# Products of a zero tile ahead of the first row tile, and another landing time for the first transfers in the planner

## The chip, the cores and the metric

One NeuronCore of a Trainium2 chip runs the kernel; one launch computes one decoder layer for 1024 tokens. The metric is the device time of an execution in microseconds (us), the median of several. A profile of one execution shows what each engine did: TensorE (PE, with its weight loads as PEld), VectorE (DVE), ScalarE (ACT), GpSimd (POOL), and SyncE (SP), which issues the transfers.

## The reference

The layer has 1024 rows (tokens) of 1024 columns. What matters here is its beginning: a row-wise normalisation of `x` and the product with `w_in`.

```
def rmsnorm(x, g):
    y = x * lax.rsqrt(jnp.mean(x * x, axis=-1, keepdims=True) + EPS)
    return y * g

a = rmsnorm(h, ln_pre_mix)               # h = x, (1024, 1024)
q, k, v, u, z = jnp.split(a @ w_in, splits, axis=-1)
attn = dilated_attention(q, k, v)
sgu = spatial_gating(u, z, sgu_ln_g, sgu_ln_b, w_spatial, b_spatial)
groups = jnp.concatenate([rmsnorm(attn, attn_out_norm), rmsnorm(sgu, sgu_out_norm)], axis=-1)
h = h + rmsnorm(groups @ w_out, ln_post_mix)
g, up = jnp.split(rmsnorm(h, ln_pre_ffn) @ w_gate_up, 2, axis=-1)
h = h + rmsnorm((silu(g) * up) @ w_down, ln_post_ffn)
h = h + sigmoid(h @ w_pe_gate + b_pe_gate) * (p @ w_pe_proj)
```

## The kernel before, in words

**How it is written and ordered.** `hybrid_block` does not issue instructions. It records every operation in a `Graph` (`G.call`, with `pe` and `load` as short forms for TensorE and for a transfer), with the buffers that the operation reads and writes. When all is recorded, `Graph.order` simulates the five engines with a price for each operation (`price`) and picks, for each engine whenever it is free, the first recorded operation that is ready and whose buffers fit; `Graph.issue` then writes the instructions in the picked order, all from line 383, which is why every row of the profile names L383. What an engine gets is therefore a fixed list, which it works off in order. A transfer is planned to land at `dma + 3.0` us (line 328), where `dma` is the time at which the planned transfers before it and its own bytes are through. Buffers come from pools that are named in the profile: `m` (4 KB per partition), `s` (2 KB), `t` (a few columns), `p` (a bank of PSUM), `c` (constants).

**The beginning of the program.** The gain row `ln_pre_mix` is loaded into one partition (`g_raw`, an `m`), and a row of ones (`ones`, an `s` of one partition, set by a memset on DVE) spreads it over 128 partitions: two f32 products `ones` x `g_raw` of 512 columns each (line 622), which DVE copies from PSUM into `g_pre` (line 623). The profile shows each f32 product of this kind as two records of 512 columns. After the gain row, SP issues row tile 0 of `x` (128 rows, 512 KB), the identity `ident`, row tile 1, the four blocks of `w_in` for the values (512 KB each) and further row tiles between them.

`x_chain(t)` (line 627) treats a row tile: ACT squares it and sums the squares, ACT and POOL make the reciprocal root from the sum (`rstd_from`, the POOL row `t<-t,c`), DVE scales the two halves of the tile by it and by `g_pre` (the `SCALAR_TENSOR_TENSOR` rows), and `Feat.first` turns each half with four transposes on PE against `ident` (rows `p<-c,s`, 128x128; "turns" below). ACT copies the two turned halves from PSUM for later use (`COPY m<-p`), then casts them to the rounded type in which PE multiplies (four `CAST m<-p`), and DVE subtracts to keep the remainder (four `TENSOR_TENSOR m<-p,m`). `split_raw` does the same for a block of `w_in`: a cast on ACT (`CAST m<-m`) and a subtraction on DVE or POOL (`TENSOR_TENSOR m<-m,m`). `v_out` then multiplies: three products for each pair of such parts, 512 columns wide (rows `MATMUL p<-m,m`).

On ACT's list the first cast of `w_in` stands ahead of the two copies of row tile 0, the four casts of the turned tile stand behind the copies, and behind these the cast of the second half of the same block, which POOL's first subtraction reads.

Of the kernel before, what the change touches and what calls it, by code (L numbers as in the profile page):

```python
# [17 lines left out]
P = 128  # L18
# [95 lines left out]
class Graph:  # L114
# [109 lines left out]
    def order(self):  # L224
        ops = self.ops
        n = len(ops)
# [17 lines left out]
        port, dma, table, lanes = 0.0, 1.5, 0, [0.0] * 8  # L244
# [4 lines left out]
        def release(o):  # L249
            ready = {}  # L250
            for e in o.engines:
                ready[e] = max([d.end + (LATENCY[e] if d.engine != e else 0.0) for d in o.deps], default=0.0)
                if e in ("tensor", "vector") and o.deps:
                    own = [d for d in o.deps if d.engine == e]
                    other = [d.end + LATENCY[e] for d in o.deps if d.engine != e]
                    ready[e] = max(other + [d.start + d.cost[e][0] for d in own], default=0.0)
                    o.sure = max(other, default=-1.0) + self.MARGIN
                heapq.heappush(coming, (ready[e], o.rank, o.i, e))
                heapq.heappush(events, ready[e])
                if e == "tensor":  # L260
                    heapq.heappush(events, ready[e] + self.MARGIN)
            o.ready = ready
# [19 lines left out]
        def pick(e, now):  # L282
            best = None
            front = ops[first]
            for rank, i in waiting[e][: self.LOOK[e]] + [(front.rank, first)] * ((front.rank, first) in waiting[e]):
                o = ops[i]
                if o.port[e] and port > now + 1e-9:
                    continue
                if best is not None and o.sure > now:
                    continue  # L290
                if not fits(o, now):
                    continue
                if e != "tensor" or o.sure <= now:
                    return o
                best = o
            return best
# [6 lines left out]
        while left:  # L303
            if not events:
                raise ValueError(f"stuck at {ops[first].what} {first}")
            now = heapq.heappop(events)
            while events and events[0] <= now + 1e-9:
                heapq.heappop(events)
            while coming and coming[0][0] <= now + 1e-9:
                _, rank, i, e = heapq.heappop(coming)  # L310
                if ops[i].start is not None:
                    continue
                bisect.insort(waiting[e], (rank, i))
            for e in engines:
                if at[e] > now + 1e-9 or not waiting[e]:
                    continue
                o = pick(e, now)
                if o is None:
                    continue
                busy, took = o.cost[e]  # L320
                o.start, o.engine = now, e
                picked.append(o)
                if o.table and o.table != table:
                    busy, took, table = busy + 1.4, took + 1.4, o.table
                at[e] = now + busy
                if e == "sync":
                    dma = max(dma, now + 0.4) + o.bytes / 330e3
                    o.end = dma + 3.0
                    lanes = lanes[1:] + [o.end]
                    at[e] = max(at[e], lanes[0])  # L330
                else:
                    o.end = now + took
                if o.port[e]:
                    port = o.end
                    heapq.heappush(events, port)
                for x in o.engines:
                    if (o.rank, o.i) in waiting[x]:
                        waiting[x].remove((o.rank, o.i))
                o.new = [b for b in o.bufs if b.slot is None]
                for b in o.new:  # L340
                    b.slot = heapq.heappop(free[b.kind])[1]
                    group[b.group] = group.get(b.group, 0) + 1
                    b.ahead = first
                    early[b.kind][first : b.born] += 1
                for b in o.bufs:
                    b.left -= 1
                    b.until = max(b.until, o.end)
                    if not b.left:
                        heapq.heappush(free[b.kind], (b.until, b.slot))
                        group[b.group] -= 1  # L350
                        live[b.kind][b.born : b.last + 1] -= 1
                        early[b.kind][b.ahead : b.born] -= 1
                        heapq.heappush(events, b.until)
                done[o.i] = True
                left -= 1
                while first < n and done[first]:
                    first += 1
                for u in o.users:
                    u.waits -= 1
                    if not u.waits:  # L360
                        release(u)
                heapq.heappush(events, at[e])
                heapq.heappush(events, now + 0.02)
# [25 lines left out]
def hybrid_block(ctx: ExitStack, tc, a, out):  # L389
    G = Graph()  # L390

    def M(dt=F32, shape=(P, 1024), group=None):
        return G.buf("M", shape, dt, group)

    def SM(dt=F32, shape=(P, 512), group=None):
        return G.buf("S", shape, dt, group)

    def PB(shape=(P, 512), group=None):
        return G.buf("P", shape, F32, group)
# [10 lines left out]
    def pe(what, *args, **kw):  # L410
        return G.call("tensor", what, *args, **kw)
# [4 lines left out]
    def load(dst, src, rate=1.0):  # L416
        o = G.call("sync", "dma_start", dst, src)
        o.bytes /= rate
        return o
# [179 lines left out]

    x = a["x"][0]  # L600
    g_raw, g_pre = M()[:1, :], M()
    ones = SM()[:1, :P]
    G.call("vector", "memset", ones, 1.0)
    load(g_raw, a["ln_pre_mix"])
    xts = {}

    def x_load(t):
        xts[t] = M()
        load(xts[t], x[t * P : (t + 1) * P, :])
# [7 lines left out]
    wv_raw.append(load_raw(piece_a(w_in, 1024, 1), None))  # L617
    for t in range(4, 6):
        x_load(t)
    for cs in (LO, HI):  # L620
        ps = PB()
        pe("matmul", ps, ones, g_raw[:, cs], start=True, stop=True)
        G.call("vector", "tensor_copy", g_pre[:, cs], ps)

    A = Feat()

# [218 lines left out]
    def unit(pr, hh, Pq, vs, bias):  # L845
# [21 lines left out]
        for b in range(0, len(order), 3 if Pq == 2 else 2):  # L867
            ps = PB((P, 4, P), "turn")
            places, n = [], 0
            for j in order[b : b + (3 if Pq == 2 else 2)]:  # L870
                for ii in sorted(blocks[j]):
                    pe("transpose", ps[:, n + ii - min(blocks[j]), :], blocks[j][ii], ident)
                places.append((j, min(blocks[j]), n, len(blocks[j])))
                n += len(blocks[j])
            eh, el = SM(F32R, (P, 4, P)), SM(F32R, (P, 4, P))
            split(*(v.flat()[:, : n * P] for v in (eh, el, ps)))
            for j, i0, at, w in places:
                for s, ee in ((0, eh), (1, el)):
                    pe("matmul", po[:, i0 * P : (i0 + w) * P], vs[j], ee.flat()[:, at * P : (at + w) * P],
                       start=j == order[0] and s == 0, stop=j == order[-1] and s == 1)  # L880
# [343 lines left out]
    for q in ORDER:  # L1224
# [3 lines left out]
        for g in range(NG):  # L1228
            for j, c in USED.get(q, ()):
                cs = slice(c * 512, (c + 1) * 512)  # L1230
# [5 lines left out]
            if g % 2 == 0:  # L1236
                n = min(2, NG - g)
# [102 lines left out]
```

## Time and profile before

| | |
|---|---|
| median of 3 runs | 1178.31 us (1178.01 to 1178.48) |
| the profiled execution | 1178.0 us |
| its span, first to last instruction | 1176.2 us |
| PE busy | 1163.5 us, 99% of the span |
| DVE, ACT, POOL busy | 869.0, 576.3, 57.0 us |
| PE's share of the chain that ended last | 95% |

The span is the time in the trace; the execution's own time is 1.8 us longer. The busy time of an engine says how full it is, not what it holds up. For a change at the start of the program the views to read are the chain that ended last in its first part, which tells what released what, and the timeline of each engine over the first 15 us, where every row has its start, its length, the engine, the operation with its tiles, a count, and in brackets the idle time ahead of it with what ended it. Rows with the same operation that follow each other are merged, and the count says how many there are.

### The profile page before, as it was taken

How to read it: one execution, taken by the hardware profiler on the slowest of the kernel's cores; microseconds unless marked ns; L12 is line 12 of the kernel's file. 1: busy time of each engine (PE TensorE's matmuls, PEld its weight loads, DVE VectorE, ACT ScalarE, POOL GpSimd, SP SyncE). 2: the span in 40 equal slices, each digit the busy share in tenths (PEclk: the TensorE clock that was granted, in tenths of full speed). 3: DMA queues.
4: the chain of work that ended last, by engine and by line, in shares of the span. 5: the costliest groups of instructions: out<-in, count | busy, mean ns of one | idle time of the engine just before them, and what ended most of it. 6: DMA issues, size and time to landing. Idle time of an engine off the chain costs nothing.

```text
span 1176.2 us, 16341 instructions
## 1 busy us (share of the span) xinstructions
PE 1163.5 (99%) x5633; PEld 972.4 (83%) x5633; DVE 869.0 (74%) x1703; ACT 576.3 (49%) x1300; POOL 57.0 (5%) x68
## 2 busy tenths in 40 slices
PE   8999999999999999999999999999999999999998
PEld 6887888788878888888888888888888888888887
DVE  7888796566666676799888888887668965479653
ACT  8663436578768666566223222222344445357121
POOL 2101000000121000310000000000000000002000
PEclk9999999999999999999999999999999999999999
DMA  8224136999763996388455656544397223643111
GB/s 295 81 72 122 58 134 192 323 296 310 250 215 88 286 264 179 109 267 256 146 194 186 196 189 186 171 133 162 112 382 254 95 92 113 240 162 143 47 43 54
DMA packets 161244, 208.77 MB, mean 177 GB/s; under 512 B 12477, under 2 KB 89609, under 8 KB 161162
## 3 DMA queue, kind: packets, MB, share of 16 engines
q1 hardware_dynamic: 161162, 207.74, 55.4%
q8 instruction: 44, 0.72, 0.3%
q14 instruction: 38, 0.31, 0.1%
HBM read 147.63 MB, written 60.06 MB: 177 GB/s over the span
## 4 chain that ended last, share of the span: by engine, by line
PE 95%; DVE 2%; ACT 1%; DMA 1%; issue 0%; SPq 0%; POOL 0%; DVEq 0%; ACTq 0%
PE p L383 95%; DVE s L383 1%; ACT m L383 1%; DMA m<-in_w_in 1%; DVE t L383 1%; DMA d<-m 0%; DVE m L383 0%; SPq L383 0%; POOL m L383 0%; ACT s L383 0%; ACT t L383 0%; DVEq L383 0%; ACTq L383 0%
## 5 line engine op out<-in xcount | busy, mean ns | idle before, releaser
L383 PE MATMUL p<-m,m 128*128 128x512 f32 (+2 forms) x4620 | 1065.6, 388 | 1.9 <-DVE m L383 1.3
L383 PEld LDWEIGHTS p<-m,m 128*128 128x128 f32 x4620 | 848.0, 188 | 169.8 <-ACT m L383 2.0
L383 DVE TENSOR_TENSOR m<-m,m 128x512 fp32r<-128x512 f32 (+2 forms) x465 | 313.2, 707 | 70.5 <-ACT m L383 65.0
L383 ACT CAST m<-m 128x512 fp32r<-128x512 f32 x363 | 212.7, 622 | 192.8 <-PE p L383 148.1
L383 DVE TENSOR_TENSOR s<-p,s 128x512 f32<-128x512 f32 (+4 forms) x222 | 143.0, 655 | 85.9 <-PE p L383 58.4
L383 ACT ACTIVATE s<-s 128x512 f32<-128x512 f32 (+1 forms) x71 | 44.3, 626 | 218.0 <-DVE s L383 162.3
L383 DVE TENSOR_TENSOR m<-p,m 128x256 fp32r<-128x256 f32 (+3 forms) x132 | 61.5, 493 | 41.2 <-PE p L383 21.5
L383 POOL TENSOR_TENSOR t<-t,c 128x1 f32<-128x1 f32 (+1 forms) x56 | 42.0, 755 | 1012.4 <-ACT t L383 1002.9
L383 ACT COPY s<-p 128x512 f32<-128x512 f32 (+1 forms) x122 | 62.2, 517 | 44.0 <-PE p L383 43.0
L383 ACT CAST m<-s 128x256 fp32r<-128x256 f32 (+1 forms) x121 | 53.6, 480 | 29.3 <-PE p L383 15.6
L383 DVE TENSOR_TENSOR s<-s,s 128x512 f32<-128x512 f32 x88 | 60.7, 692 | 4.6 <-ACT s L383 0.7
L383 DVE TENSOR_TENSOR m<-s,m 128x256 fp32r<-128x256 f32 (+1 forms) x121 | 58.4, 511 | 6.9 <-ACT m L383 6.5
L383 PE MATMUL p<-c,m 128*128 128x128 f32 x328 | 49.7, 273 | 0.0
L383 ACT COPY m<-p 128x512 f32<-128x512 f32 (+1 forms) x72 | 31.5, 452 | 32.1 <-PE p L383 30.9
L383 PE MATMUL p<-c,s 128*128 128x128 f32 (+2 forms) x249 | 42.6, 282 | 2.4 <-DVE s L383 2.0
L383 PEld LDWEIGHTS p<-c,m 128*128 128x128 f32 x328 | 39.5, 140 | 5.9
L383 PE MATMUL p<-s,m 128*128 128x128 f32 (+1 forms) x256 | 43.8, 276 | 0.0
L383 ACT ACTIVATE m<-m 128x1024 f32<-128x1024 f32 x32 | 34.1, 1068 | 19.5 <-DVE m L383 15.0
L383 PEld LDWEIGHTS p<-c,s 128*128 128x128 f32 (+2 forms) x249 | 32.0, 145 | 11.4 <-DVE s L383 4.0
L383 PEld LDWEIGHTS p<-s,m 128*128 128x128 f32 x256 | 38.1, 190 | 3.2
L383 ACT ACTIVATE m<-m,t 128x384 f32<-128x384 f32 (+2 forms) x64 | 36.7, 578 | 4.9 <-DVE t L383 4.3
L383 ACT CAST m<-p 128x256 fp32r<-128x256 f32 (+1 forms) x80 | 34.4, 498 | 6.7 <-PE p L383 5.7
(58 smaller groups left out, 513.9 us busy)
## 6 DMA issues: line engine op xcount, KB each, us to landing
d<-s SPq DMA_DIRECT2D x149, 256.0 KB, 2.8
m<-d SPq DMA_DIRECT2D x51, 512.0 KB, 4.2
m<-in_w_gate_up SPq DMA_DIRECT2D x88, 256.0 KB, 3.9
m<-d SPq DMA_DIRECT2D x87, 256.0 KB, 7.2
s<-d SPq DMA_DIRECT2D x56, 256.0 KB, 4.2
d<-m SPq DMA_DIRECT2D x28, 512.0 KB, 5.4
m<-in_w_down SPq DMA_DIRECT2D x44, 256.0 KB, 6.1
m<-in_w_in SPq DMA_DIRECT2D x20, 512.0 KB, 3.9
```

The costliest lines, as they stand in the source:

```text
L383: getattr(getattr(nc, o.engine), o.what)(*[real(v) for v in o.args], **{k: real(v) for k, v in o.kw.items()})
```

## The change

A tile `unused` of 128x512 zeros is set by a memset on DVE. A new helper, `keep_busy(n)`, multiplies the tile by itself `n` times (f32, 512 columns) into a bank of PSUM that nobody reads. It is called once ahead of the two products with `ones`, and twice behind them; the latter are recorded to come after the second product with `ones`. In the planner, a transfer that is issued in the first 12 us of the plan lands 1.7 us after its bytes in place of 3.0.

```
@@ Graph.order @@
                     dma = max(dma, now + 0.4) + o.bytes / 330e3
-                    o.end = dma + 3.0
+                    o.end = dma + (3.0 if now > 12 else 1.7)
                     lanes = lanes[1:] + [o.end]
...
@@ hybrid_block @@
     g_raw, g_pre = M()[:1, :], M()
-    ones = SM()[:1, :P]
+    ones, unused = SM()[:1, :P], SM()
+    G.call("vector", "memset", unused, 0.0)
     G.call("vector", "memset", ones, 1.0)
     load(g_raw, a["ln_pre_mix"])
     xts = {}
+
+    def keep_busy(n, after=()):
+
+        ps = PB()
+        for _ in range(n):
+            pe("matmul", ps, unused[:, :P], unused, start=True, stop=True, after=after)
...
     for t in range(4, 6):
         x_load(t)
+    keep_busy(1)
     for cs in (LO, HI):
         ps = PB()
-        pe("matmul", ps, ones, g_raw[:, cs], start=True, stop=True)
+        o = pe("matmul", ps, ones, g_raw[:, cs], start=True, stop=True)
         G.call("vector", "tensor_copy", g_pre[:, cs], ps)
+    keep_busy(2, [o])
```

TensorE at the start of the program, before. In the names, `s_144` is `ones`, `m_142` is `g_raw`, `c_73` is `ident`; the first two groups of four are the turns of row tile 0.

```order
L383 MATMUL p_161<-m_142,s_144 128x512
L383 MATMUL p_163<-m_142,s_144 128x512
L383 MATMUL p_188<-c_73,s_184 128x128 x4
L383 MATMUL p_201<-c_73,s_186 128x128 x4
L383 MATMUL p_214<-c_73,s_205 128x128 x4
L383 MATMUL p_227<-m_199,m_220 128x512
```

TensorE at the same place, now. `s_144` is here `unused`, and `s_148` is `ones`.

```order
L383 MATMUL p_150<-s_144 128x512
L383 MATMUL p_163<-m_142,s_148 128x512
L383 MATMUL p_167<-m_142,s_148 128x512
L383 MATMUL p_176<-s_144 128x512 x2
L383 MATMUL p_195<-c_73,s_191 128x128 x4
L383 MATMUL p_208<-c_73,s_193 128x128 x4
L383 MATMUL p_221<-c_73,s_212 128x128 x4
L383 MATMUL p_234<-m_206,m_227 128x512
```

One product of zeros stands ahead of the products with `ones`, two stand between these and the turns of row tile 0; the rest of the list is that of before.

VectorE at the start of the program, before: the memset of a constant, that of `ones`, the two copies of the gain row, the scaling of row tile 0.

```order
L383 MEMSET c_72 128x8
L383 MEMSET s_144 1x128
L383 COPY m_165<-p_161 128x512
L383 COPY m_165<-p_163 128x512
L383 SCALAR_TENSOR_TENSOR s_184<-m_146,t_177,m_165 128x512
```

VectorE at the same place, now.

```order
L383 MEMSET c_72 128x8
L383 MEMSET s_144 128x512
L383 MEMSET s_148 1x128
L383 COPY m_169<-p_163 128x512
L383 COPY m_169<-p_167 128x512
L383 SCALAR_TENSOR_TENSOR s_191<-m_146,t_184,m_169 128x512
```

The memset of `unused` stands ahead of that of `ones`; nothing else on VectorE moves. The lists of ScalarE, GpSimd and SyncE are row for row those of before, with other buffer numbers, and they are so too with the landing of 3.0 left as it was.

## Rows read from the trace of the kernel before

**Rows 1.** The page, busy time of each engine, share of the span and number of instructions.
```profile
PE 1163.5 (99%) x5633; PEld 972.4 (83%) x5633; DVE 869.0 (74%) x1703; ACT 576.3 (49%) x1300; POOL 57.0 (5%) x68
```

**Rows 2.** The chain that ended last, in order of time, its first 60 us: start, length, what.
```profile
2.49 7.05 DMA m<-in_w_in
9.54 0.02 issue
9.56 3.21 ACT m L383 x8
12.78 0.07 issue
12.85 1.29 POOL m L383
14.14 0.04 issue
14.18 45.85 PE p L383 x224
```

**Rows 3.** The timeline of the first 22 us, rows of ACT from the first cast of weights on, and POOL's first subtraction: start, length, engine, line, operation, count, idle time before it and its releaser.
```profile
9.56 0.62 ACT L383 CAST m<-m 128x512 fp32r<-128x512 f32 x1 [0.92 <-DMA m<-in_w_in]
10.09 1.07 ACT L383 COPY m<-p 128x512 f32<-128x512 f32 x2
...
11.04 1.21 ACT L383 CAST m<-p 128x256 fp32r<-128x256 f32 x4
...
12.10 1.71 ACT L383 CAST m<-m 128x512 fp32r<-128x512 f32 x3
...
12.85 1.28 POOL L383 TENSOR_TENSOR m<-m,m 128x512 fp32r<-128x512 f32 x1 [3.56 <-ACT m L383]
...
13.65 1.12 ACT L383 COPY m<-p 128x512 f32<-128x512 f32 x2
```

**Rows 4.** The same timeline, rows of PE and, where they show single records, of its weight loads.
```profile
2.43 3.75 PE L383 MATMUL p<-m,s 1*128 1x512 f32 x4 [2.43 <-DMA m<-in_ln_pre_mix]
...
3.42 0.33 PEld L383 LDWEIGHTS p<-m,s 1*128 1x128 f32 x1 [0.52 <-issue]
...
4.27 0.33 PEld L383 LDWEIGHTS p<-m,s 1*128 1x128 f32 x1 [0.52 <-issue]
...
7.62 1.97 PE L383 MATMUL p<-c,s 128*128 128x128 f32 x8 [1.44 <-DVE s L383]
...
10.12 1.11 PE L383 MATMUL p<-c,s 128*128 128x128 f32 x4 [0.53 <-DVE s L383]
...
11.48 1.22 PE L383 MATMUL p<-m,m 128*128 128x512 f32 x2 [0.24 <-ACT m L383]
...
12.50 1.05 PE L383 MATMUL p<-c,s 128*128 128x128 f32 x4
...
13.21 8.98 PE L383 MATMUL p<-m,m 128*128 128x512 f32 x36
```

**Rows 5.** Windows of 2 us: length, busy time and instructions of PE, PEld, DVE, ACT, POOL, the granted clock of TensorE as a share of full speed, the share of the DMA engines, GB/s.
```profile
2.00:4.00 2.00, 1.57 (x2) 0.83 (x3) 0.00 (x0) 0.01 (x1) 0.00 (x0) 1.00 0.82 259
...
8.00:10.00 2.00, 1.59 (x8) 1.19 (x6) 0.91 (x2) 1.05 (x4) 0.56 (x1) 1.00 1.05 411
10.00:12.00 2.00, 1.63 (x5) 1.22 (x6) 1.43 (x3) 2.00 (x7) 0.00 (x0) 1.00 1.02 415
```

**Rows 6.** The timeline of PE from 14.6 to 40 us.
```profile
14.18 8.00 PE L383 MATMUL p<-m,m 128*128 128x512 f32 x34
22.02 0.60 PE L383 MATMUL p<-c,s 128*128 128x128 f32 x4
...
25.22 1.03 PE L383 MATMUL p<-c,s 128*128 128x128 f32 x8
```

**Rows 7.** The timeline of the first 22 us, rows of DVE up to the scaling of row tile 1, and POOL's first row of the reciprocal root.
```profile
0.81 0.07 DVE L383 MEMSET c<- 128x8 f32 x1 [0.81 <-PEq L1328]
0.85 0.17 DVE L383 MEMSET s<- 1x128 f32 x1
...
4.51 0.69 DVE L383 COPY m<-p 128x512 f32<-128x512 f32 x1 [3.50 <-PE p L383]
...
6.22 0.69 DVE L383 COPY m<-p 128x512 f32<-128x512 f32 x1 [1.01 <-PE p L383]
6.22 0.55 POOL L383 TENSOR_TENSOR t<-t,c 128x1 f32<-128x1 f32 x1 [5.78 <-ACT t L383]
...
6.83 1.41 DVE L383 SCALAR_TENSOR_TENSOR s<-m,t,m 128x512 f32<-128x512 f32 x2
...
9.32 0.75 DVE L383 SCALAR_TENSOR_TENSOR s<-m,t,m 128x512 f32<-128x512 f32 x1 [1.09 <-POOL t L383]
```

## The prediction

> **What bounds the kernel now.** I read the page's busy line first. TensorE (PE) is busy for 1163.5 of 1176.2 us [rows 1], so a change at the start can gain only what PE loses there, and it can cost whatever delays the point from which PE never waits again. The second view is the chain that ended last, over its first 60 us [rows 2]. The reader should see what stands ahead of PE's first long stretch: the transfer of a block of `w_in` (2.49 to 9.54), eight ScalarE (ACT) instructions from 9.56, one GpSimd (POOL) subtraction from 12.85 to 14.13, and then PE from 14.18. No PE instruction stands in that chain before 14.18.
>
> The third view is the timeline, taken engine by engine. ACT waits 0.92 us for the block of `w_in`, starts at 9.56, and from there on its rows touch or overlap: a cast of weights, two copies of the turned row tile out of PSUM (10.09), four casts of it (11.04), and three casts of weights (12.10) [rows 3]. The first of those three makes the weights' second half, and POOL's 1.28 us subtraction waits for it. PE's rows before 14.18 [rows 4] are short bursts: the four records of the two products with `ones` (2.43 to 6.18), the eight turns of row tile 0 (7.62 to 9.59), the four turns of 10.12, two products, four turns, three products.
>
> The clock of these bursts has to be read from their pace. The column of the granted clock says 1.00 for these stretches [rows 5], but eight turns take 1.97 us at 7.62 [rows 4] and the same eight-turn row takes 1.03 us at 25.22; four take 1.11 or 1.05 early and 0.60 at 22.02 [rows 6]. That is a factor of nearly two between equal rows, so I read the early stretch as the lower level, 1.2 GHz, up to the turns of 12.50 at least, and 2.4 GHz in the 34 products from 14.18, which follow each other every 0.235 us (8.00 us over 34) [rows 6].
>
> **The change part by part.** *The landing in the planner.* The 1.7 in place of 3.0 moves a due time in the planner and no instruction: the order on all five engines is that of before, except for the memset on VectorE (DVE) and the three products on PE. It costs and gains nothing.
>
> *The memset of the zero tile.* It stands on DVE ahead of the memset of `ones`. 8 columns took 0.07 us and 128 took 0.17 [rows 7]: 0.10 us for 120 columns, so 512 columns come to 0.49 us by the slope and to 0.68 by four times the larger row. I take 0.5, because the slope leaves the fixed part in once. The memset of `ones` then ends near 1.5 (at most 1.7), and what hides it is the landing of `ln_pre_mix`, for which PE waits until 2.43 [rows 4]. Cost: nothing.
>
> *The first zero product.* It waits for that memset, so it starts at 0.85 + 0.5 + 0.05 = 1.4 (at most 1.55). Behind it in PE's queue stand the two products with `ones`. One f32 product is two records here (four for two [rows 4]). From PE's start at 2.43 to the weight load of 3.42 are 0.99 us and to the next 0.85, so one product takes 1.84 at the lower clock and ends at 3.25 to 3.4. The `ones` products therefore start 0.8 to 0.95 late; I take 0.85. The last result comes at 7.03 in place of 6.18, the second copy of `g_pre` on DVE [rows 7] starts at 7.07 in place of 6.22, and the two scalings of row tile 0 start at 7.67 in place of 6.83, since DVE takes its instructions in order. Turns could then begin at 8.47 in place of 7.62. If the clock rises while the `ones` products run, this shrinks, but it can gain nothing: the scaling also needs POOL's power, which runs from 6.22 to 6.77 [rows 7].
>
> *The two later zero products.* They are four records: 4 x 0.85 = 3.4 us at 1.2 GHz, half of it, 1.7, at 2.4. They start where the last `ones` record lets PE go: 4.27 + 0.85 + 0.85 = 5.97 before, 6.82 with the delay. PE is free for the turns at 10.2 if nothing has risen, and at w + (10.2 - w)/2 if the clock rises at time w.
>
> *Who waits for the turns.* ACT's copies at 10.09 and, half of 1.07 later, at 10.6 [rows 3] read the eight turns. Before, the turns ended at 9.59, behind which the first copy could have run; it did not, because the weights' cast in front of it waited for its transfer. So faster or earlier turns do not start the copies earlier. With the turns at the higher clock (four in 0.60, eight in 1.03) they are in time if PE is free by 9.5. That is w + (10.2 - w)/2 = 9.5, so w = 8.8: **if the clock has risen by 8.8, the edit costs nothing.** What of PE's later rows before 14.18 becomes faster ends earlier and waits for POOL's 14.13 as before. The gain there is nothing too: PE's start at 14.18 has POOL, ACT and the transfer behind it, none of which PE feeds late.
>
> *Sum.* 0 + 0 + 0 - 0 against the profiled execution's 1178.0 us (span 1176.2 and 1.8 around it), so 1178.0 by its own account. The three runs shown have a median of 1178.31, that is 0.3 above it, and reach from 1178.01 to 1178.48. I forecast **1178.2**: no change, between the two.
>
> **The rivals.** *The clock stays low, and the zero products are late (slower).* The `ones` records kept PE without a gap for 3.75 us, and the turns after them still ran at 1.2 GHz [rows 4]; so that the f32 products of zeros raise it is not shown by any row. Then PE is free at 10.2, the first four turns end 1.11 later at 11.3, the eight 1.97 later at 12.2, and the second copy starts at 12.2 in place of 10.6. ACT, POOL and PE's 14.18 move by 1.6: **1179.6** from the profiled execution, 1179.9 from the median. It decides from w = 8.8 upwards. It passes 0.2% (2.36 us) only if the clock also stays low after PE's new start at 15.8: products at half pace until 17.3 would add the missing 0.76. Against this rival: PE would now work without a gap from 1.4 on, 7.4 us by the point that decides, and in the trace the clock rose between the turns of 12.50 and the products of 14.18, after a stretch from 10.12 on with one gap of 0.24 [rows 4, 6].
>
> *The rise is late in other executions of before (faster).* In the profiled one the clock was up by the products of 14.18, just in time. Where it rises d later, PE does half the work in d and loses d/2, and an engine kept busy from 1.4 would not. The runs shown bound it: the slowest is 0.47 above the fastest, so d is at most about 0.9, and against the median the gain is 0.3: **1178.0**; a median one microsecond lower would need d near 2, which no run shown has. The Trainium skill ("TensorE: Matmul & The Clock Gate", Part 1: The HAM clock gate) has a rule for this: the throttled clock is the default, activity releases it, and the same kernel is seen with different numbers of slow matmuls from run to run. By that rule this rival holds for some executions and the spread of before would narrow; the trace has one execution and cannot show it.
>
> *The turns are on the path after all (faster).* Then PE's rows between 10.12 and 14.18, 1.11 + 1.22 + 1.05 + 0.97 (13.21 to 14.18) = 4.35 us at the lower clock, would halve: 2.2 us, **1175.8** by the profiled execution. Against it speak ACT's rows without a gap from 9.56 and the chain, which names no PE before 14.18 [rows 2, 3].
>
> *The change does not do what it says.* As to the order this is so for the landing, as told above: it changes no row. That is in the forecast already and makes no time of its own.
>
> **How the numbers follow.** Forecast (no change, 1178.0 to 1178.6): 0.55. Zero products late (1178.7 to 1180.7, with the middle at 1179.6 to 1179.9): 0.26, of which 0.05 go beyond 0.2%. Late rise in before (1177.0 to 1178.0): 0.13. Turns on the path: 0.03. Left over: 0.03, other waits of the start that I have not seen, of either sign. A measurement of this kernel can tell about 0.2%, 2.36 us, from no change. So faster by over 0.2%: 0.03; slower by over 0.2%: 0.05; within: 0.92. The range takes in the late rise down to 1177.3 and the late zero products up to 1180.0 (1.6 above the median, and 0.1 for the dearer memset), and leaves some 0.2 outside.
>
> **What would show it.** Right: in the profile after, PE works from about 1.4; the eight turns take near 1.03 us and end by 10.6; ACT's first weight cast still starts at about 9.56 and its copies follow without a gap; POOL's subtraction and PE's long stretch still start near 12.85 and 14.18. The clock rising by 8.8 shows as weight loads or turns at half the spacing. Wrong: an idle gap on ACT between its weight cast and its copies, ended by PE (the late zero products), with PE's long stretch starting after 15; or the long stretch starting well before 14.18, which would mean that the chain named the wrong engine; or ACT's first cast starting at another time, since no term of mine moves the transfer.

## The result, and the profile after

| | before | changed |
|---|---|---|
| median | 1178.25 us (17 runs, 1177.18 to 1180.51) | 1181.22 us (17 runs, 1179.92 to 1184.48) |
| ratio to before | | 1.0024, 95% interval 1.0016 to 1.0031 |
| the profiled execution | 1178.0 | 1180.71 |
| its span | 1176.2 | 1178.9 |

The change costs 2.8 us by the ratio (1.9 to 3.7 by its interval), 3.0 by the medians. The forecast was no change, 1178.2, and its range ended at 1180.0. The ratios here and below leave out one run of e7_front that took 3833 us.

The timeline of the changed kernel's first 22 us, rows of PE and of those who wait for it, answers to [rows 3, 4, 7]; the columns are the same.

```profile
0.94 0.61 DVE L383 MEMSET s<- 128x512 f32 x2
...
1.49 2.08 PE L383 MATMUL p<-s 128*128 128x512 f32 x2 [1.49 <-DVE s L383]
...
3.49 3.78 PE L383 MATMUL p<-m,s 1*128 1x512 f32 x4
...
7.20 3.78 PE L383 MATMUL p<-s 128*128 128x512 f32 x4
7.30 0.69 DVE L383 COPY m<-p 128x512 f32<-128x512 f32 x1 [1.02 <-PE p L383]
...
8.53 0.62 ACT L383 CAST m<-m 128x512 fp32r<-128x512 f32 x1 [0.74 <-DMA m<-in_w_in]
...
10.77 2.75 PE L383 MATMUL p<-c,s 128*128 128x128 f32 x12
...
11.87 0.59 ACT L383 COPY m<-p 128x512 f32<-128x512 f32 x1 [2.72 <-PE p L383]
...
12.72 0.59 ACT L383 COPY m<-p 128x512 f32<-128x512 f32 x1 [0.27 <-PE p L383]
...
14.20 0.60 PE L383 MATMUL p<-c,s 128*128 128x128 f32 x4
...
15.00 1.27 POOL L383 TENSOR_TENSOR m<-m,m 128x512 fp32r<-128x512 f32 x1 [6.58 <-ACT m L383]
...
16.33 5.97 PE L383 MATMUL p<-m,m 128*128 128x512 f32 x25 [0.85 <-POOL m L383]
```

PE has no idle time from 1.49 to 13.5, and its records go at the pace of the lower level: the four records of the later zero products take the same 3.78 us as the four of the products with `ones`, and twelve turns take 2.75 us (0.21 each), until four turns at 14.20 take 0.60. The turns start at 10.77 in place of 7.62. ACT, which before had no gap behind its first cast of weights, now idles 2.72 and 0.27 us ahead of its two copies, both times until PE. From there everything is shifted by the same amount: the second copy from near 10.6 (the second half of the row at 10.09) to 12.72, POOL's subtraction from 12.85 to 15.00, PE's long stretch from 14.18 to 16.33, the last two by 2.15 us. PE looks fuller, and that says nothing: the page has it busy 1168.2 us against 1163.5 [rows 1].

```profile
PE 1168.2 (99%) x5639; PEld 973.6 (83%) x5639; DVE 868.9 (74%) x1704; ACT 576.7 (49%) x1300; POOL 56.7 (5%) x68
```

The chain that ended last in the first 60 us of the changed kernel answers to [rows 2].

```profile
2.49 6.02 DMA m<-in_w_in
...
8.55 6.42 issue
...
15.00 1.28 POOL m L383
16.29 0.04 issue
16.33 43.84 PE p L383 x215
```

Here the chain misleads: it follows POOL's wait on ACT to an "issue" of 6.42 us. The timeline shows what fills it: ACT waiting for the turns, that is for PE's zero products. The span grew by 2.7, and 2.15 of it lie ahead of the long stretch.

The transfer of the first block of `w_in` landed at 8.5 here and at 9.54 in the trace of before, though nothing ahead of it on SP's list changed. This turns out to matter below.

### The profile page after: what moved, and what is told of

Its sections match the earlier page's. It is cut to its first block, busy times and chain, and to the rows that moved or that the text cites. A ratio compares the mean times of both kernels' runs of the same rounds, so it can differ in the third digit from the quotient of the medians.

```text
span 1178.9 us, 16356 instructions
## 1 busy us (share of the span) xinstructions
PE 1168.2 (99%) x5639; PEld 973.6 (83%) x5639; DVE 868.9 (74%) x1704; ACT 576.7 (49%) x1300; POOL 56.7 (5%) x68
## 4 chain that ended last, share of the span: by engine, by line
PE 94%; DVE 2%; DMA 1%; ACT 1%; issue 1%; SPq 0%; POOL 0%; ACTq 0%; POOLq 0%; DVEq 0%
PE p L383 94%; DVE s L383 1%; ACT m L383 1%; DMA m<-in_w_gate_up 1%; DMA m<-in_w_in 1%; DVE t L383 1%; DMA d<-m 0%; DVE m L383 0%; SPq L383 0%; POOL m L383 0%; ACT s L383 0%; ACT t L383 0%; ACTq L383 0%; POOLq L383 0%; DVEq L383 0%
```

## The experiments

For each: the median, the ratio to before with its 95% interval, and from the profile of one of its runs the start of ACT's first cast of weights (right behind the landing of the first block of `w_in`), of the turns of row tile 0, and of PE's long stretch. Each ratio is to runs of before taken in the same series, whose medians were 1178.07 to 1178.25 (1178.52 for e9_casts_first).

| run | median us | ratio (interval) | ACT's cast | turns | long stretch |
|---|---|---|---|---|---|
| before, first trace | | | 9.56 | 7.62 | 14.18 |
| b_again | one run | | 8.68 | 7.64 | 13.29 |
| changed, first trace | 1181.22 | 1.0024 (1.0016 to 1.0031) | 8.53 | 10.77 | 16.33 |
| a_again | one run | | 8.90 | 10.42 | 15.16 |
| e0_landing | 1178.06 | 1.0003 (0.9994 to 1.0012) | 8.42 | 7.52 | 13.14 |
| e1_first | 1178.82 | 1.0007 (0.9998 to 1.0015) | 8.55 | 8.71 | 14.33 |
| e2_later | 1179.61 | 1.0018 (1.0009 to 1.0027) | 8.96 | 9.60 | 14.89 |
| e3_four | 1181.67 | 1.0036 (1.0024 to 1.0049) | 9.16 | 12.26 | 16.99 |
| e4_data | 1181.20 | 1.0027 (1.0017 to 1.0036) | 8.97 | 10.77 | 16.04 |
| e5_rounded | 1180.99 | 1.0021 (1.0012 to 1.0030) | 8.57 | 10.78 | 16.33 |
| e7_front | 1180.30 | 1.0016 (1.0006 to 1.0025) | 8.47 | 10.52 | (14.51) |
| e8_one_later | 1178.83 | 1.0005 (0.9996 to 1.0014) | 8.92 | 7.91 | 13.53 |

(e6_turns, whose zero turns share a row with the real ones, and e9_casts_first are told in their places. In e7_front PE does not wait for POOL, and its last burst starts at 14.51.)

**e0_landing: the planner's half alone.**

```
-                    o.end = dma + 3.0
+                    o.end = dma + (3.0 if now > 12 else 1.7)
```

> Only the planner's landing time is changed (1.7 in place of 3.0 for the first 12 us), no product of zeros. Theory (the loss is the zero products on PE's list, ahead of the turns): the lists of all engines are those of before, so the time is that of before, 1178.3, ratio 1.000 within 0.001, and PE's long stretch starts near 14.2. Rival (the other landing itself costs): 1179.5 or more.

1178.06 against 1178.07 of before: the landing time in the planner costs nothing that can be told (the interval ends at 1.4 us). The rows of every engine in its trace stand in the order of before, so it is also a further trace of the lists of before.

**e1_first and e2_later: one call of `keep_busy` each.**

e1_first:

```
-    keep_busy(2, [o])
```

> The change with the first zero product alone; the two later ones are left out. Theory: the products with ones come 1.06 us late, the turns begin near 8.7 in place of 7.6, their eighth ends near 10.4, and ACT's second copy, at 10.6 before, hardly waits; PE's long stretch starts at 14.0 to 14.4, time 1178.3 (at most 1178.7). Rival (the late gain row is part of the loss): a third to a half of the loss stays, 1179.3 or more, with DVE's scaling as the releaser.

e2_later:

```
-    keep_busy(1)
```

> The change with the two later zero products alone; the first is left out. Theory: all at 1.2 GHz, the zero products start at 6.14 and free PE at 9.7, 1.06 before the changed kernel; the second copy starts at 11.7, PE's long stretch at 15.3; 1.1 us above before, 1179.4. Rival (the loss is not PE's queue but the products as such): as the changed kernel, 1181. A rise of the clock before 9 would give 1178.3.

The run e2_later is near its theory: turns at 9.60, 1179.61, and by the ratio 2.1 us above before, where the theory had 1.1, the lower end of the interval. The run e1_first is between theory and rival: 1178.82, with 1.0 within the interval. ACT's copies waited 0.69 and 0.27 us for the turns, since the block landed at 8.5 in that execution; the long stretch at 14.33 is about a microsecond later than the 13.14 and 13.29 of the traces of before with a landing near it. With a landing at 9.54 ACT's copies could not run before 10.09, so the same late turns would cost next to nothing; that is worked out, and no trace of e1_first has it. By the ratios the two halves cost 0.8 and 2.1 us, which add up to the 2.8 of the whole as well as the intervals can tell.

ACT in the first 17.5 us of e1_first:

```profile
9.86 0.59 ACT L383 COPY m<-p 128x512 f32<-128x512 f32 x1 [0.69 <-PE p L383]
10.71 0.59 ACT L383 COPY m<-p 128x512 f32<-128x512 f32 x1 [0.27 <-PE p L383]
```

**e3_four: four later zero products.**

```
-    keep_busy(2, [o])
+    for i in range(4):
+        z = pe("matmul", ps, unused[:, :P], unused, start=True, stop=True, after=[o])
+        z.cost = z.cost if i < 2 else {"tensor": (0.001, 0.001)}
```

> The change with four later zero products in place of two (the two more are priced at next to nothing in the planner, so that the lists stay as they are otherwise). Theory with the clock held low by them until the end: turns 3.4 us later than in the changed kernel, PE's long stretch at 19.7, 5.6 us above before, 1183.8. With the clock rising near 13.4 as in both traces: long stretch at 18.4, 1182.5. Rival (PE's queue does not decide): as the changed kernel, 1181.

1181.67, below both numbers: the clock rose during the zero products, sooner than in the first trace of the changed kernel. The eight records took 5.23 us (below), where four take 3.78 at the lower level and eight would take 7.2, so the last 2 us of them ran at double pace and the rise is near 10.3. By the time alone the rival is not out, since the interval (1.0024 to 1.0049) overlaps that of the changed kernel (1.0016 to 1.0031). The trace decides: the turns start at 12.26, 1.5 to 1.8 later than in the two traces of the changed kernel, ACT's first copy waits 3.12 us for them, and the long stretch starts at 16.99 in place of 16.33 and 15.16. PE's queue decides.

PE and ACT in the first 17.5 us of e3_four:

```profile
7.20 5.23 PE L383 MATMUL p<-s 128*128 128x512 f32 x8
...
12.26 1.47 PE L383 MATMUL p<-c,s 128*128 128x128 f32 x12
...
12.90 1.07 ACT L383 COPY m<-p 128x512 f32<-128x512 f32 x2 [3.12 <-PE p L383]
```

**e4_data, e5_rounded, e6_turns: other work in the zero products' place.** None of the results is read by anybody.

e4_data:

```
-    keep_busy(2, [o])
+    for _ in range(2):
+        pe("matmul", ps, xts[0][:, :P], xts[0][:, LO], start=True, stop=True, after=[o])
```

> The two later products multiply row tile 0 of x by itself in place of zeros, still f32; nobody reads the result. Theory Z (the zeros are why the clock stayed low): the clock rises during these products, the turns run at 2.4 GHz (eight in 1.03 us) and start by 9.7; long stretch at 14.2 to 15.2, 1178.5 to 1179.5. Theory F (f32 products do not raise it, whatever the data): as the changed kernel, turns from 10.8 at 1.97 for eight, 1181. Theory G (it rises near 13.4 whatever PE does): as F.

e5_rounded:

```
-    ones, unused = SM()[:1, :P], SM()
+    ones, unused = SM()[:1, :P], SM(F32R)
...
-    keep_busy(1)
+    keep_busy(4)
...
-    keep_busy(2, [o])
+    keep_busy(8, [o])
```

> The zero tile is of the rounded type and the products are four and eight in place of one and two (one record of about 0.43 us each at 1.2 GHz, so the same time at that clock). Theory F: the clock rises during them, the eight then take 0.23 each, turns at 2.4 GHz before 9.5; long stretch at 14.2, 1178.3, at best 0.3 below before. Theories Z and G: the clock stays low to 13, turns from about 10.6, 1181.

e6_turns:

```
-    keep_busy(2, [o])
+    for i in range(16):
+        pe("transpose", ps[:, i % 4 * P : (i % 4 + 1) * P], unused[:, :P], ident, after=[o])
```

> The two later products are replaced by sixteen turns of the zero tile (16 x 0.213 = 3.4 us at 1.2 GHz), the first product of zeros stays. Theory F (f32 products do not raise the clock; in both traces it rose with turns in the stretch ahead): the clock rises near the end of the sixteen or before, the turns of row tile 0 run at 2.4 GHz, long stretch at 15 to 15.6, 1179.3 to 1180. Theories Z and G: all at 1.2, turns of row tile 0 from 10.6, 1181.

Neither the zeros of the later products (Z) nor the f32 format (F) explains a low clock at 8.8. With real data the twelve turns started at 10.77, the same time; they took 2.06 in place of 2.75, so the rise fell near 12.0. With rounded zeros there was no rise until the turns were nearly through (2.67 for twelve). With turns as filler, 28 turns in a row took 4.79 us, where twelve take 2.75 at the lower level and 28 would take 6.2, so the rise was near 10.4. The median of e6_turns was 1181.35, ratio 1.0024 (1.0015 to 1.0033), as the changed kernel.

PE in the first 17.5 us of e4_data:

```profile
10.77 2.06 PE L383 MATMUL p<-c,s 128*128 128x128 f32 x12
```

Of e5_rounded:

```profile
10.78 2.67 PE L383 MATMUL p<-c,s 128*128 128x128 f32 x12
```

Of e6_turns:

```profile
7.20 4.79 PE L383 MATMUL p<-c,s 128*128 128x128 f32 x28
```

In all traces so far the rise lay between 10 and 14, whatever PE ran from 7.2 on. Two explanations were left: nothing raises the clock before 10, or what PE ran before 7.2 did not help.

**e7_front: four zero products in one piece, ahead of the products with `ones`.**

```
-    keep_busy(1)
+    for i in range(4):
+        z = pe("matmul", ps, unused[:, :P], unused, start=True, stop=True)
+        z.cost = z.cost if i < 1 else {"tensor": (0.001, 0.001)}
...
-    keep_busy(2, [o])
```

> Four zero products (eight records) ahead of the products with ones, none behind; the three more are priced at next to nothing in the planner, the lists are otherwise as before. Theory H (the clock rises late in the changed kernel because the one-row products with ones stand between the zero products; zeros without a break raise it sooner): the clock rises between 4.6 and 8.1, the records then go at 0.43 each, the ones products are through by about 9.3, the turns run at 2.4 GHz from 10.8, long stretch near 15.7, 1180 to 1180.5. Theory G (it does not rise before 10.3 whatever PE does): ones products from 8.6 to 12.3, turns from 13.7, long stretch near 18.6, 1183.

PE in the first 17.5 us of e7_front:

```profile
1.48 5.68 PE L383 MATMUL p<-s 128*128 128x512 f32 x8 [1.48 <-DVE s L383]
...
7.09 1.98 PE L383 MATMUL p<-m,s 1*128 1x512 f32 x4
...
10.52 2.02 PE L383 MATMUL p<-c,s 128*128 128x128 f32 x12 [1.44 <-DVE s L383]
...
13.80 1.05 PE L383 MATMUL p<-c,s 128*128 128x128 f32 x4
```

What theory H says of the clock holds in this trace: eight records took 5.68 in place of 7.2, so the rise is near 5.5, after 4 us of zero products, and the four records with `ones` took 1.98 in place of 3.75. Its long stretch at 15.7 did not come so: the last burst starts at 14.51, at the lower level again. The kernel was slower than before all the same (1.0016): with four zero products ahead of the products with `ones`, the turns start at 10.52 and not at 7.62, and ACT's copies wait for them. The higher level did not last: PE idled 1.44 us for DVE's scaling, and the four turns at 13.80 took 1.05 again. The windows of the same run show the granted clock there (columns as in [rows 5]):

```profile
10.00:12.00 2.00, 1.47 (x9) 1.00 (x10) 2.00 (x4) 0.72 (x2) 0.00 (x0) 1.00 1.03 413
12.00:14.00 2.00, 1.75 (x7) 1.18 (x7) 1.73 (x5) 2.00 (x7) 0.00 (x0) 0.58 1.06 400
14.00:16.00 2.00, 2.00 (x9) 1.46 (x8) 2.00 (x5) 2.00 (x6) 1.29 (x1) 0.56 1.05 416
```

**e8_one_later: one zero product behind the products with `ones`, none ahead.**

```
-    keep_busy(1)
...
-    keep_busy(2, [o])
+    keep_busy(1, [o])
```

> One zero product behind the products with ones, none ahead. Theory (only what passes the slack of ACT's copies costs): the product lies between 6.1 and 8.0 at 1.2 GHz, the turns start 0.4 late; where the block of w_in lands near 9.5 this costs nothing, where it lands near 8.4 it costs 0.4: 1178.1 to 1178.5. Rival (every zero product costs its length): 1.8 above before, 1179.9.

1178.83, interval of the ratio 0.9996 to 1.0014, and the long stretch at 13.53, 4.6 behind the cast as in before: what fits into the slack costs nothing that these runs can tell, while 1.8 us (1.0015) lies outside the interval.

**b_again, a_again: further traces of both kernels.**

> The kernel before, another look. Theory (PE's long stretch begins where the landing of the first block of w_in puts it): if the block lands at t, ACT's first cast starts right behind and the long stretch starts at t + 4.6 to t + 4.8 (9.54 and 14.18 in the first trace), whenever the clock rises as long as that is before; the clock rises between 10.3 and 13.7. Rival (the turns decide before as well): the long stretch starts at 14.2 whatever the landing.

> The changed kernel, another look. Theory: the turns start at 10.8 if the clock has not risen by then, a little earlier if it rises between 10.3 and 10.8; ACT's copies wait for them whatever the landing of w_in (8.4 to 9.8); long stretch 15.3 (clock up at 10.3) to 16.4 (clock up at 13.4 or later). Rival: the long stretch follows the landing, t + 7.8 as in the first trace.

In before, cast and long stretch are 4.6 to 4.7 us apart in all three traces of its lists (9.56 and 14.18, 8.68 and 13.29, 8.42 and 13.14): the landing decides. In the changed kernel they are 7.8 and 6.3 apart; there the turns decide, and they start at 10.77 or, with the rise during the zero products (3.39 us for the four records in place of 3.78, so near 10.0), at 10.42. From the timeline of a_again:

```profile
7.20 3.39 PE L383 MATMUL p<-s 128*128 128x512 f32 x4
...
8.90 0.62 ACT L383 CAST m<-m 128x512 fp32r<-128x512 f32 x1 [0.52 <-DMA m<-in_w_in]
...
10.42 1.47 PE L383 MATMUL p<-c,s 128*128 128x128 f32 x12
...
11.06 1.07 ACT L383 COPY m<-p 128x512 f32<-128x512 f32 x2 [1.55 <-PE p L383]
```

From that of b_again, the same place:

```profile
8.68 0.62 ACT L383 CAST m<-m 128x512 fp32r<-128x512 f32 x1 [0.59 <-DMA m<-in_w_in]
...
9.20 1.07 ACT L383 COPY m<-p 128x512 f32<-128x512 f32 x2
```

**e9_casts_first: a try at a faster kernel.** If ACT's list sets the long stretch, the two copies for later use should not stand in it. For row tile 0 they were recorded behind the casts; no zero products.

```
-                copy(self.half[t // 2 * 2][j][:, t % 2], ps.flat())
+                if t or self is not A:
+                    copy(self.half[t // 2 * 2][j][:, t % 2], ps.flat())
                 self.put(1 + j, t, ps)
+                if self is A and not t:
+                    copy(self.half[t // 2 * 2][j][:, t % 2], ps.flat())
```

> The kernel before, without zero products; for row tile 0 alone the four casts of the turned tile and the weights' cast stand ahead of the two copies that are for later use (1.07 us). Theory (ACT's list from the landing t of the first block of w_in to the weights' second cast sets PE's long stretch, t + 4.6): POOL's subtraction starts about 1 us sooner after the landing, long stretch at t + 3.6, 1 us below before, 1177.1, if PE finds work behind it. Rival (the order behind it changes too and PE waits again before 30 us): long stretch sooner, but the same time, 1178.2.

1179.36 against 1178.52, ratio 1.0007 (0.9998 to 1.0016): no gain. ACT's first cast started at 9.22 and POOL's subtraction at 11.53, 2.3 us behind it in place of 3.3, as the theory wants. But part of what PE did sooner ran at the lower clock (eleven products took 3.89 us, where 0.235 each would be 2.6), the planner's order behind it changed too, PE waited again at 41.35, and by the wait that ends at 104.06 in before and 104.63 here the kernel was 0.6 behind. The gain is given back, and which of these took how much is not separated; no run beat the kernel before by more than the noise.

ACT, PE and POOL in the first 17.5 us of e9_casts_first:

```profile
9.22 0.62 ACT L383 CAST m<-m 128x512 fp32r<-128x512 f32 x1
...
11.53 3.89 PE L383 MATMUL p<-m,m 128*128 128x512 f32 x11
11.53 1.29 POOL L383 TENSOR_TENSOR m<-m,m 128x512 fp32r<-128x512 f32 x1 [1.61 <-ACT m L383]
```

## Why the prediction was wrong, point by point

**What bounds the start of before: right.** The transfer, ACT's list and POOL set PE's 14.18: in three traces the long stretch follows ACT's first cast by 4.6 to 4.7 us. That faster turns alone would bring nothing is argued from this and not shown; no run has them without a delay.

**The landing in the planner, the memset: right.** e0_landing has 1.0003; the memset of 512 columns took 0.49 us and the first zero product began at 1.49, within the 1.4 to 1.55.

**The first zero product: hidden in the trace I had, not in all.** I gave it 0.85 us of delay and a cost of nothing, with ACT's copies at 10.09 as cover. The delay was 1.06. The cover was a property of one execution: its block of `w_in` landed at 9.54, while those of the thirteen other traces landed between 8.4 and 9.7, six of them below 8.7. It moves without the change: the lists of before have 8.4 in e0_landing and 9.54 in the first trace. So ACT's first cast at 8.53, a sign that I had named for being wrong, tells nothing against the terms. With a landing at 8.5 the first copy could run at 9.1, and turns that begin at 8.71 are late (0.69 and 0.27 us of waiting in e1_first).

**The two later zero products: the step that failed.** They cost nothing in the forecast because the clock was to have risen by 8.8, and I held that for likelier than not, because PE would work without a gap from 1.4 on. It did work so, and in no trace of the kernel with both calls of `keep_busy`, nor of its variants with other work in the later place, had the clock risen before 10. The products with `ones`, with one row of weights each, lie between 3.49 and 7.2, and the rise came only behind the start of the second piece, at 7.20: some 2.8 us later at the soonest and some 6 us at the latest. e7_front shows, in one trace, that it is the arrangement: zeros in one piece raised the clock after 4 us. I had a sign of it in the trace and put it into the rival: 3.75 us of these same products had left the turns at 1.2 GHz. With the second piece starting at 7.20, the soonest rise seen, near 10.0, is already behind the 9.5 by which PE had to be free. Which property of the products with `ones` matters was not tried.

The condition was too easy as well. With PE free at 10.77 at the lower level, as measured, the same sum gives a rise by 8.2 and not by 8.8. And with a landing at 8.5 not even a rise at 7.20 would do: PE would be free at 9.0 and the first four turns through at 9.6, where the first copy could run at 9.1. That is worked out from these rows; no run has such a rise with this list.

**The rival that came true was under-sized.** I had PE free at 10.2 and 1.6 us of loss. The first zero product took 2.00 us (1.49 to 3.49) where I had 1.84, the four records with `ones` 3.71 (3.49 to 7.20) where I had 3.54, the four later ones 3.57 (7.20 to 10.77) where I had 3.4, and the first started at 1.49 and not at 1.4. So PE came free at 10.77. That is 0.57 more and gives the 2.15 of the first two traces. The landing moves this number: against traces of before at 13.14 and 13.29, the changed kernel's 15.16 and 16.33 are 1.9 to 3.2 later. The mean of three traces of before (13.54) and of two of the changed kernel (15.75) differ by 2.2, which lies in the interval of 1.9 to 3.7. Behind the long stretch both traces of the changed kernel have some 0.5 us more than those of before (last section); that these belong to the change is not shown, and the rest up to 2.8 stays open.

**The late rise in before as a gain: did not show.** The clock rose before the long stretch in every trace of before. The Trainium skill ("TensorE: Matmul & The Clock Gate", Part 1: The HAM clock gate) has the moment of the rise vary from run to run; the two traces of the changed kernel, near 10.0 and after 13, agree.

## What to carry to other kernels

Filler work on an in-order engine is work ahead of whatever is queued behind it: it needs an end that is safe at the lower clock, not at the one that it is meant to bring about. Slack read from one trace is slack of that execution; when what stands ahead of it is a transfer, look at a second trace before leaning on it. And before buying a higher clock, ask who would use it: here the work that it sped up had another engine's list and a transfer in front of the point that mattered.

## What the runs showed of the hardware

The first block's landing moved by 1.3 us between executions of programs whose issues ahead of it are the same (8.4 to 9.7).

Also, the clock falls once more in the middle of some executions. Near 329 us PE waits twice for DVE, 0.73 and 0.79 us, in both kernels. In e0_landing ten products behind these waits took 4.15 us, in the first trace of before 2.56; the windows show the clock granted at half.

The timeline of PE in the first trace of before:

```profile
329.48 2.56 PE L383 MATMUL p<-m,s 128*128 128x512 f32 x10 [0.79 <-DVE s L383]
```

The same in e0_landing:

```profile
328.94 4.15 PE L383 MATMUL p<-m,s 128*128 128x512 f32 x10 [0.79 <-DVE s L383]
```

The window of 330 to 332 us in the first trace of before, with the columns of [rows 5]:

```profile
330.00:332.00 2.00, 2.00 (x11) 1.62 (x11) 1.83 (x5) 1.42 (x3) 1.63 (x1) 1.00 1.02 254
```

The same window in e0_landing:

```profile
330.00:332.00 2.00, 2.00 (x6) 1.60 (x5) 1.28 (x4) 0.88 (x3) 1.06 (x1) 0.50 1.04 244
```

From the long stretch to the span's end are 1162.0 us in the first trace of before and 1162.1 in b_again, but 1164.1 in e0_landing and 1164.6 in a_again, which both have this stretch: it costs about 2 us in them, nearly as much as the change. It is not what makes the changed kernel slower. The mean granted clock of a run tells who has it: it is 0.998 in the seven traces in which the clock fell on the way (in e7_front at the start) and 0.999 or more in the seven others. By this mark 6 of the 17 runs of the changed kernel have it and 21 of the 89 runs of before in the series of the experiments. The medians are 1181.92 and 1179.09 with it, 1180.71 and 1177.84 without it, so the change costs 2.8 and 2.9 us. Whether one kernel meets it more often stays open.

The first trace of the changed kernel does not have it; it has 1162.6, with 0.26 us of idle PE ahead of 434.74, where the chain that ended last names a block of `w_gate_up` (6.21 us). a_again has 0.42 us of idle PE ahead of 402.29, for another transfer, and its 1164.6 is 0.5 above e0_landing. No trace of before has either wait. Of the variants with filler in both places e6_turns has one like the first (0.32 us ahead of 435.28), and e3_four and e5_rounded have none (1162.1 and 1162.0), so whether the change brings them is not shown. From the timeline of the changed kernel's first trace:

```profile
434.74 0.73 PE L383 MATMUL p<-m,m 128*128 128x512 f32 x2 [0.26 <-ACT m L383]
```
